# Ten slot tiles instead of twelve in a mixture-of-experts kernel: places of 96 and 64 slots, filled in the order of the token counts

## The chip, the cores and the metric

The kernel runs on one core of a Trainium2 chip. The metric is the device time of one execution in microseconds (us). Before the change three runs took 1160.12, 1155.77 and 1158.53 us, a median of 1158.53 us.

## What is computed

A two-layer transformer on 512 tokens of width 1024, float32. Each layer is attention (layer 0: block-sparse plus differential, layer 1: compressed, selected and windowed) and then a mixture of 16 experts. The change touches the mixture alone:

```python
def hier_moe(h, wg, bg, we, be, w_gate, w_up, w_down):      # t: 512 tokens x 1024
    ...
    _, gsel = lax.top_k(gl, 1)                              # one of 4 groups of 4 experts
    ...
    tv, ti = lax.top_k(el_g, MOE_TOPK)                      # 2 experts of that group
    tw = jax.nn.softmax(tv, axis=-1)
    ...
    a = jax.nn.silu(jnp.einsum('td,edf->tef', t, w_gate)) * jnp.einsum('td,edf->tef', t, w_up)
    y = jnp.einsum('tef,efd->td', a * comb[:, :, None].astype(a.dtype), w_down)
```

So 1024 (token, expert) pairs are spread over 16 experts of 256 hidden units. An expert's weights are 3 MiB: 1 MiB gate, 1 MiB up, 1 MiB down.

## The kernel before

Both layers run the same program for the mixture (`Moe.run`). Each expert has a place of `CAP` = 96 slots; the 16 x 96 = 1536 slots are cut into 12 slot tiles of 128 rows, that is four quarters of 32 rows each, so a tile holds rows of two experts (quarter q of tile t belongs to expert (4t + q) // 3, `groups`). For a tile t the steps are:

- `place_tile` (one-hot matrices on VectorE at L1310, small matmuls at L1317 and L1321, `indices`): which token sits in which slot. Then `gather` (L1232, GpSimd) fetches the 128 token rows from DRAM; the first tile is built by matmuls instead (`r0`, L1340).
- `normed_rows` (ScalarE, L1248) scales the rows into `xs`, `rows_T` transposes them on TensorE (L1259) into `xT`.
- `up` (L1269): 8 steps over the width and in each step four matmuls, one per quarter, each against gate and up of that quarter's expert. A whole `up`, 32 matmuls in the program, is one row of 64 in the trace. `silu` and product give `sg` (L1272, L1275).
- `down`: `sg` transposed (L1282), 16 matmuls (L1291, a row of 32 in the trace), the rows times the tokens' weights (`tile_weight`, L1404; L1294), and `scatter` (L1302, GpSimd) to the DRAM array `yD`. The last two tiles do not scatter: their rows are added by matmuls with the transposed one-hots (`combine`, L1549). `add_rows` reads `yD` back (`yr`, SP, L1534) and adds it (L1538, L1539).

TensorE runs them as: up(t+1), placing of a later tile, down(t). The order on each engine is chosen by a scheduler at build time, not written out; the program only gives the order of emission and some pins.

The weights come by DMAs that SP issues (`Experts`): per expert four half-MiB DMAs for gate and up (L1059) and one of 1 MiB for down (L1065). There are buffers for `GUB` = 5 experts of gate and up, in two halves, and for `DNB` = 4 experts of down. A buffer is free when the last matmul that reads it is done: SP then waits at that DMA, and everything behind it in SP's queue waits too.

If an expert has more than 96 tokens, the kernel runs `overflow` for it (L1416 on) inside an If (L1474) between up(2) and up(3), `IF_AT` = 2. Every engine loads the largest count, `cmaxi`, and branches. In this execution the body of that branch was not run.

Of the kernel before, what the change touches and what calls it, by code (L numbers as in the profile page):

```python
# [25 lines left out]
SLOT_TILES = NEXP * CAP // 128  # L26
# [11 lines left out]
IF_AT = 2  # L38
TAIL_AT = 8
# [35 lines left out]
def hybrid_kernel(ctx: ExitStack, tc: tile.TileContext, A: dict, out: bass.AP, dbg=None):  # L75
# [970 lines left out]
    class Experts:  # L1046


        def __init__(self, pool, l):
            self.pool, self.l, self.gu, self.dn = pool, l, {}, {}  # L1050
# [11 lines left out]
        def down(self, e):  # L1062
            if e not in self.dn and e < NEXP:
                self.dn[e] = self.pool.tile([128, 2, D], F32, name="dn", tag="dn", bufs=DNB)
                nc.sync.dma_start(self.dn[e], A["moe_w_down"][self.l, e].rearrange("(p j) c -> p j c", j=2))  # L1065
# [106 lines left out]
    def moe(l, m, done):  # L1172
        s2, b2, nD, yD = m.s2, m.b2, m.nD, m.yD
        with mkpool(f"mx{l}") as mp, mkpool(f"moe{l}", "right") as fp:
# [9 lines left out]
            for j in range(XGB):  # L1184
# [3 lines left out]
            PIECES = {0: ((0, 0, 0, 96), (1, 0, 96, 32)), 1: ((1, 32, 0, 64), (2, 0, 64, 64)),  # L1188
                      2: ((2, 64, 0, 32), (3, 0, 32, 96))}
            SPAN = {0: (0, 2), 1: (1, 3), 2: (2, 4)}  # L1190
# [5 lines left out]
            for h in range(2):  # L1196
# [7 lines left out]
                for i in range(2 * h, 2 * h + 2):  # L1204
                    for e, s0, o, n in PIECES[0]:
# [12 lines left out]
            for q in (1, 2):  # L1218
                nc.gpsimd.tensor_tensor(rsr, rs[:, :NT] if q == 1 else rsr, rsp[:, :, q - 1], op=ALU.subtract)
                nc.gpsimd.tensor_copy(rsp[:, :, q], rsr)  # L1220

# [84 lines left out]
            def place_tile(t, pinned=False):  # L1306
                b, j = t // 3, t % 3
                OH[t] = fp.tile([128, NT, 128], BF, name="oh", tag="oh", bufs=XGB + 3)
                for e, s0, o, n in PIECES[j]:
                    nc.vector.tensor_tensor(OH[t][:, :, o:o + n],  # L1310
                                            rm[:, :, 4 * b + e:4 * b + e + 1].to_broadcast([128, NT, n]),
                                            iotas[:, None, s0:s0 + n].to_broadcast([128, NT, n]), op=ALU.is_equal)
                lo, hi = SPAN[j]
                cd = cod[:, :, 4 * b + lo:4 * b + hi]
                tb = ps("P" if t in PLB else "O")
                for i in range(NT):
                    o = nc.tensor.matmul(tb[:, 0:8], OH[t][:, i, :], cd[:, i].rearrange("p e c a -> p (e c a)"),  # L1317
# [3 lines left out]
                    nc.tensor.matmul(tb[:, 8:11], OH[t][:, i, :], rsp[:, i, :], start=False, stop=(i == NT - 1),  # L1321
                                     skip_group_check=True)
                IX[t] = sm([128, 2], f"ix{t}", I32)
                indices(tb[:, 0:8].rearrange("p (e c a) -> p e c a", e=2, c=2), IX[t], segm[:, j, lo:hi])
                RSL[t] = sm([128, 1], f"rsl{t}")
                nc.vector.tensor_reduce(RSL[t], tb[:, 8:11], axis=AX.X, op=ALU.add)
# [49 lines left out]
            for q in range(3):  # L1376
                nc.vector.tensor_copy(wc[:, :, :, q], wv)
                if q < 2:
                    nc.vector.tensor_tensor(wv, wv, wc[:, :, :, q], op=ALU.subtract)
            cmax = sm([128, 1], "cmax")  # L1380
# [305 lines left out]
```

## Time and profile before

| | |
|---|---|
| median of 3 runs | 1158.53 us |
| the profiled execution | 1158.82 us |
| its span, first to last instruction | 1157.1 us |
| mean granted TensorE clock | 0.963 |
| TensorE busy | 1056.2 us, 91% |
| mixture of layer 0, first `up` to the last `down` | 369.05 to 528.96 us |
| mixture of layer 1, first `up` to the last `down` | 976 to 1139.3 us |

The profiled execution was 1158.82 us, of which 1.72 us lie outside the span. Times in the trace count from the span's start. A row of a timeline gives start, duration, engine, line, operation, out<-in, count, and in brackets the idle time before it with what ended it. Busy TensorE is measured in matmuls whose ends are modelled, so the starts are what is read here. An engine name with a q behind it is that engine's own instruction queue.

### The profile page before, as it was taken

The page shows a single profiled execution, that of the slowest core. Times are in us where ns is not written, and L with a number is a line of the kernel's source. Part 1 is how long each engine was busy: PE and PEld are TensorE (multiplying, and loading weights), DVE is VectorE, ACT ScalarE, POOL GpSimd, SP SyncE. Part 2 cuts the span into 40 slices and gives each one's busy share as a digit, 9 for nine tenths or more (in the row PEclk, how much of TensorE's full clock was granted, in tenths as well). Part 3 has the DMA queues.
Part 4 walks back from the last instruction along what each step waited for, and adds up shares of the span by engine and source line. Part 5 has one row for each costly group of instructions (what it writes and reads, how often), then busy time and mean ns, then how long its engine had stood idle before and what let it go on. Part 6 is the DMA issues. An engine that isn't in the chain of part 4 may idle for free. (4 is left out here: it accounts for less than half of the span.)

```text
span 1157.1 us, 21456 instructions
## 1 busy us (share of the span) xinstructions
PE 1056.2 (91%) x8123; PEld 729.7 (63%) x8124; DVE 598.9 (52%) x1651; ACT 512.5 (44%) x1277; POOL 275.9 (24%) x355
## 2 busy tenths in 40 slices
PE   5899899989998999996999997995999998999994
PEld 3798889978773433334999976763678673433332
DVE  2575869775325332338327587547564225332337
ACT  3235565765442222224334674674755542313222
POOL 2110011332222211212101242233324323211214
PEclk9989999999998999998999998998999998999997
DMA  8864647541196889855376265005012094989853
GB/s 272 293 191 147 200 147 225 196 147 56 55 382 212 310 328 412 329 190 166 76 192 227 79 202 173 15 16 139 27 37 74 12 396 183 309 336 416 319 202 125
DMA packets 114212, 225.98 MB, mean 195 GB/s; under 512 B 31694, under 2 KB 75662, under 8 KB 108976
## 3 DMA queue, kind: packets, MB, share of 16 engines
q1 hardware_dynamic: 104832, 203.85, 51.4%
q0 software_dynamic: 7776, 20.07, 4.6%
q8 instruction: 68, 1.11, 0.4%
q10 hardware_dynamic: 1488, 0.55, 0.2%
q14 instruction: 48, 0.39, 0.1%
HBM read 212.73 MB, written 18.93 MB: 200 GB/s over the span
## 5 line engine op out<-in xcount | busy, mean ns | idle before, releaser
L343 PE MATMUL psP<-wh,hTh 128*128 128x256 f32 (+1 forms) x656 | 190.1, 295 | 12.1 <-ACT raw L456 6.3
L343 PE MATMUL psP<-wl,hTh 128*128 128x256 f32 (+1 forms) x656 | 184.8, 292 | 6.5 <-DVE wl L312 6.4
L343 PE MATMUL psP<-wh,hTl 128*128 128x256 f32 (+1 forms) x656 | 187.9, 290 | 0.1
L1269 PE MATMUL psS<-gu,xT 128*32 128x512 f32 x1536 | 175.9, 603 | 0.3
L343 PEld LDWEIGHTS psP<-wh,hTh 128*128 128x128 f32 x656 | 128.3, 197 | 15.1 <-ACT raw L456 7.1
L343 PEld LDWEIGHTS psP<-wl,hTh 128*128 128x128 f32 x656 | 125.5, 195 | 9.8 <-DVE wl L312 8.9
L509 DVE CUSTOM_DVE_ANT_0 P<-psS,cmask 128x128 f32<-128x128 f32 x192 | 87.3, 487 | 85.7 <-PE psS L505 51.8
L518 POOL TENSOR_SCALAR P<-P,sm 128x128 f32<-128x128 f32 (+3 forms) x160 | 94.3, 609 | 150.2 <-DVE sm L957 72.2
L343 PEld LDWEIGHTS psP<-wh,hTl 128*128 128x128 f32 x656 | 127.7, 195 | 3.4 <-issue 2.5
L310 ACT CAST wh<-w 128x512 fp32r<-128x512 f32 (+1 forms) x124 | 75.2, 608 | 116.7 <-PE psP L343 74.7
L510 ACT ACTIVATE P<-P,nm 128x128 f32<-128x128 f32 x192 | 107.4, 561 | 37.6 <-DVE nm L509 37.1
L312 POOL TENSOR_TENSOR wl<-w,wh 128x512 fp32r<-128x512 f32 (+1 forms) x38 | 52.5, 1383 | 283.2 <-ACT wh L310 236.2
L1269 PEld LDWEIGHTS psS<-gu,xT 128*32 128x32 f32 x1536 | 55.3, 111 | 99.7 <-issue 90.9
L234 DVE SCALAR_TENSOR_TENSOR g<-w,cs,g 128x512 f32<-128x512 f32 x140 | 111.0, 818 | 11.0 <-DMA w<-in_ada_w_dram 11.0
L505 PE MATMUL psS<-kT,qT 128*128 128x256 f32 (+3 forms) x384 | 95.7, 345 | 3.1 <-DVE nm L509 2.7
L343 PE MATMUL psP<-wh,o 128*128 128x256 f32 x480 | 94.1, 289 | 2.1 <-ACT o L310 1.4
L312 DVE TENSOR_TENSOR wl<-w,wh 128x512 fp32r<-128x512 f32 (+1 forms) x86 | 59.6, 693 | 67.9 <-ACT wh L310 67.1
L1291 PE MATMUL psP<-dn,sT 128*32 128x512 f32 x768 | 89.1, 603 | 1.0 <-ACT sT L1284 0.8
L173 ACT COPY PT<-psT 128x512 f32<-128x512 f32 x132 | 66.1, 511 | 46.7 <-PE psT L531 46.0
L343 PEld LDWEIGHTS psP<-wh,o 128*128 128x128 f32 x480 | 75.1, 190 | 13.3 <-issue 8.2
L531 PE MATMUL psT<-identr,P 128*128 128x128 f32 x440 | 72.5, 284 | 5.0 <-ACT PT L173 4.8
L1240 ACT ACTIVATE xT<-psT,bm,sm 128x128 f32<-128x128 f32 x96 | 36.1, 457 | 88.8 <-PE psT L1259 88.8
(338 smaller groups left out, 1729.0 us busy)
## 6 DMA issues: line engine op xcount, KB each, us to landing
w<-in_ada_w_dram SPq DMA_DIRECT2D x96, 512.0 KB
gu<-in_moe_w_gate_dram SPq DMA_DIRECT2D x64, 512.0 KB
gu<-in_moe_w_up_dram SPq DMA_DIRECT2D x64, 512.0 KB
dn<-in_moe_w_down_dram SPq DMA_DIRECT2D x32, 1024.0 KB
w<-in_ev_w_in_dram SPq DMA_DIRECT2D x20, 512.0 KB
w<-in_od_w_in_dram SPq DMA_DIRECT2D x18, 512.0 KB
yr<-yD SPq DMA_DIRECT2D x8, 1024.0 KB
w<-in_ev_w_out_dram SPq DMA_DIRECT2D x8, 512.0 KB
```

The source lines that it names most:

```text
L173: nc.scalar.copy(o, i)
L234: nc.vector.scalar_tensor_tensor(g1[:, h], t[:, h], cs[:, k:k + 1], g1[:, h], op0=ALU.mult, op1=ALU.add)
L310: nc.scalar.copy(hi, src)
L312: o = e.tensor_tensor(lo, src, hi.bitcast(F32), op=ALU.subtract)
L343: nc.tensor.matmul(dst, xx[:, k, tk], ww, start=(k == 0 and v == 0 and i % per == 0), stop=(k == 4 * len(qs) - 1 and v == 2), skip_group_c ...
L505: nc.tensor.matmul(s[:, :n], qh[:, i * 128:(i + 1) * 128], kh[:, v, :n], start=(v == 0), stop=(v == 1))
L509: nc.vector.tensor_tensor_reduce(e, s[:, :n], cmask[:, 512 - n:], -1.0, -MASKED, ALU.add, ALU.min, nm)
L510: nc.scalar.activation(e, e, AF.Exp, bias=nm, scale=-1.0, accum_out=sm[:, i:i + 1])
L518: nc.gpsimd.tensor_scalar(P[i], P[i], sm[:, i:i + 1], 1.0, op0=ALU.mult, op1=ALU.mult)
L531: nc.tensor.transpose(t[:, o:o + 128], P[i][:, j * 128:(j + 1) * 128], ident)
L1269: nc.tensor.matmul(hp[c], xT[:, k, c], gu(k), start=(k == 0), stop=(k == KC - 1), tile_position=(0, 32 * q))
L1291: nc.tensor.matmul(yp[g], sT[:, f, g], dn(f, c), start=(f == 0), stop=(f == 1), tile_position=(0, 32 * q))
```

## The change

The first five experts keep a place of 96 slots (`FIXED`). The other eleven are sorted by token count on VectorE at run time and put into eleven places whose sizes are fixed: ranks 1 to 3 get 96 slots, ranks 4 to 11 get 64, in the order of `RANKS`. 8 x 96 + 8 x 64 = 1280 slots are 10 tiles. Since the expert of a place past the fifth is only known at run time, SP loads its number (`values_load`) and the weight DMAs take their address from that register. One-hots, codes and weights of the tokens are put into the new order by products with the permutation (`reorder`). The If asks whether any place overflows and stands between up(7) and up(8) instead of between up(2) and up(3).

```diff
-SLOT_TILES = NEXP * CAP // 128
+FIXED = 5
+RANKS = (4, 5, 1, 6, 7, 2, 8, 3, 9, 10, 11)
+NSORT = NEXP - FIXED
+CAPS = (96,) * FIXED + tuple(96 if r <= 3 else 64 for r in RANKS)
+GROUPS = [(p, s) for p, n in enumerate(CAPS) for s in range(0, n, 32)]
+SLOT_TILES = len(GROUPS) // 4
+LATER = 100
...
-IF_AT = 2
-TAIL_AT = 8
+IF_AT = 7
+TAIL_AT = 6
...
+        def src(self, n, e):
+            if e < FIXED:
+                return A[n][self.l, e]
+            if e not in self.at:
+                self.at[e] = nc.values_load(self.ids[0:1, e:e + 1], engines=[mybir.EngineType.SP], min_val=FIXED,
...
+            return A[n][self.l, bass.ds(self.at[e], 1)].rearrange("o a b -> (o a) b")
...
-                        v = A[n][self.l, e].rearrange("(p k) f -> p k f", k=KC)
+                        v = self.src(n, e).rearrange("(p k) f -> p k f", k=KC)
...
+            def reorder(out, v):
+                n = v.shape[1]
+                t = row_tile()[:, 0:n * NSORT * NSORT].rearrange("p (i r e) -> p i r e", r=NSORT, e=NSORT)
+                nc.vector.tensor_tensor(t, ordr[:, None, :, :].to_broadcast([128, n, NSORT, NSORT]),
+                                        v[:, :, None, :].to_broadcast([128, n, NSORT, NSORT]), op=ALU.mult)
+                nc.vector.tensor_reduce(out, t, axis=AX.X, op=ALU.add)
+
+            def order():
+                nc.vector.tensor_copy(cnt, rk[:, 64:80])
+                nc.vector.scalar_tensor_tensor(key, cnt[:, FIXED:], float(NEXP), num, op0=ALU.mult, op1=ALU.subtract)
...
+            def reordered():
+                nc.gpsimd.tensor_copy(rmP[:, :, 0:FIXED], rm[:, :, 0:FIXED])
+                reorder(rmP[:, :, FIXED:], rm[:, :, FIXED:])
...
             def place_tile(t, pinned=False):
-                b, j = t // 3, t % 3
+                lo, hi, pieces, seg = place_of(t)
+                r, cods = (rm, cod) if hi <= FIXED else (rmP, codP)
...
             def groups(t):
-                return [weights((4 * t + q) // 3) for q in range(4)]
+                return [weights(expert_of(t, q)) for q in range(4)]
...
-                with tc.If(rv > CAP):
+                with tc.If(rv > 0):
...
             sg = up(xT0, groups(0), pinned=True)
+            with ahead(-LATER):
+                order()
+                reordered()
+                reorder_weights()
+                beyond()
...
                 if t == IF_AT:
-                    for e in range(GUB):
-                        weights.gate_up(4 * (t + 1) // 3 + e)
-                    for e in range(DNB):
-                        weights.down(4 * t // 3 + e)
+                    for e in range(done_by(t) + GUB):
+                        weights.gate_up(e)
+                    for e in range(done_by(t - 1) + DNB):
+                        weights.down(e)
```

The places of the ten tiles, quarter by quarter, are 0 0 0 1, 1 1 2 2, 2 3 3 3, 4 4 4 5, 5 6 6 7, 7 7 8 8, 9 9 10 10, 10 11 11 12, 12 12 13 13 and 14 14 15 15, counting tiles from 0. The first four tiles use 1.33 experts each; from tile 4 on it is about 1.8. The number of DMAs and of bytes of weights is unchanged.

What moves on the engines is shown at three places. First SP's queue at the start of the mixture of layer 0. The name `gu` is a half of gate and up (two halves to an expert, each with a gate and an up DMA), `dn` a down matrix. Before, with the fifth expert's `gu_4846` first and `dn_4870`, `dn_4872` those of experts 4 and 5:

```order
L1473 TENSOR_LOAD cmaxi_4464
L1059 DMA gu_4846<-in_moe_w_gate_dram 128x1024
...
L1059 DMA gu_4852<-in_moe_w_gate_dram 128x1024
...
L1065 DMA dn_4870<-in_moe_w_down_dram 128x2048
L1059 DMA gu_4858<-in_moe_w_gate_dram 128x1024
...
L1059 DMA gu_4864<-in_moe_w_gate_dram 128x1024
...
L1065 DMA dn_4872<-in_moe_w_down_dram 128x2048
L1474 COMPARE_AND_BRANCH
```

And with the change, from the load of the expert numbers on (`gu_4926` is expert 5, `dn_4924` and `dn_4935` are experts 4 and 5, `gu_5056` is expert 6, `gu_5067` expert 7):

```order
L1064 TENSOR_LOAD ids_4358
L1076 ISA
L1076 DMA gu_4926<-in_moe_w_gate_dram 128x1024
...
L1570 TENSOR_LOAD cmaxi_4365
L1570 ISA x2
L1082 DMA dn_4924<-in_moe_w_down_dram 128x2048
...
L1082 DMA dn_4935<-in_moe_w_down_dram 128x2048
...
L1076 DMA gu_5056<-in_moe_w_gate_dram 128x1024
...
L1082 DMA dn_5065<-in_moe_w_down_dram 128x2048
...
L1076 DMA gu_5067<-in_moe_w_gate_dram 128x1024
```

Before, gate and up of experts 6, 7 and 8 stand ahead of the down matrix of expert 5; now expert 6 stands behind it, expert 7 behind the down matrix of expert 6, and so on, one after the other to expert 12.

Second, VectorE between the last copy of the first tile's rows and its transposed rows `xT`. Before (`ix1_4393` is the index of tile 1, which its gather waits for):

```order
L1340 COPY w_4330<-psS_4329 128x256
...
L1228 TENSOR_REDUCE t2_4396<-t4_4394 128x2
L1229 TENSOR_SCALAR ix0_4373<-t2_4376 128x2
...
L1229 TENSOR_SCALAR ix1_4393<-t2_4396 128x2
...
L1243 TENSOR_SCALAR xT_4327<-psT_4343,sm0_3296,bm0_3302 128x128 x4
```

With the change (`ix1_4432` is that of tile 1):

```order
L1438 COPY w_4369<-psS_4368 128x256
L1294 TENSOR_TENSOR ordr_4359<-rank_4357,want_4295 128x121
...
L1283 TENSOR_TENSOR w_4562<-ordr_4359,rm_4316 128x484
...
L1283 TENSOR_TENSOR w_4567<-ordr_4359,eb_4343 128x484
...
L1283 TENSOR_TENSOR w_4571<-ordr_4359,wv_4476 128x484
L1285 TENSOR_REDUCE key_4356<-w_4557 128x11
L1342 TENSOR_SCALAR xT_4366<-psT_4382,sm0_3296,bm0_3302 128x128 x4
...
L1285 TENSOR_REDUCE rmP_4361<-w_4562 128x4x11
...
L1285 TENSOR_REDUCE ebP_4566<-w_4567 128x44
L1328 TENSOR_SCALAR ix1_4432<-t2_4435 128x2
```

The index of tile 1 stood ahead of `xT` and now stands behind it and behind three of the reductions; three products of 484 elements and the sort stand ahead of `xT`.

Third, TensorE around up(4) with the change, where the scheduler has cut it (L1368 is `up`, L1381 and L1390 are the transposes and matmuls of `down`):

```order
L1358 MATMUL psT<-identr,xs 128x128 x4
L1368 MATMUL psS<-gu,xT 32x512 x3
...
L1381 MATMUL psT<-identr,sg 128x128 x2
...
L1390 MATMUL psP<-dn,sT 32x512 x16
...
L1368 MATMUL psS<-gu,xT 32x512 x18
...
L1368 MATMUL psS<-gu,xT 32x512 x13
```

Before, every `up` ran through; now three matmuls (those of experts 5, 6 and 6) come ahead of down(3), and the fourth, of expert 7, comes behind it. The same cut stands ahead of experts 8, 10 and 12.

## Rows read from the trace of the kernel before

**Rows 1.** The page, busy time, share of the span and instructions of each engine.

```profile
PE 1056.2 (91%) x8123; PEld 729.7 (63%) x8124; DVE 598.9 (52%) x1651; ACT 512.5 (44%) x1277; POOL 275.9 (24%) x355
```

**Rows 2.** TensorE's timeline, layer 0: `up`, `down` and the weights' matmuls.

```profile
369.05 7.14 PE L1269 MATMUL psS<-gu,xT 128*32 128x512 f32 x64
...
377.44 7.17 PE L1269 MATMUL psS<-gu,xT 128*32 128x512 f32 x64
...
390.10 7.07 PE L1269 MATMUL psS<-gu,xT 128*32 128x512 f32 x64
406.39 0.24 PE L1404 MATMUL psO<-wc,oh 128*128 128x6 bf16 x4 [3.76 <-PEq L1474]
406.65 8.78 PE L1269 MATMUL psS<-gu,xT 128*32 128x512 f32 x64
...
420.73 7.07 PE L1269 MATMUL psS<-gu,xT 128*32 128x512 f32 x64
...
433.11 7.07 PE L1269 MATMUL psS<-gu,xT 128*32 128x512 f32 x64
...
499.94 3.62 PE L1269 MATMUL psS<-gu,xT 128*32 128x512 f32 x26
```

**Rows 3.** Busy time by stretch: PE, PEld, DVE, ACT, POOL, granted clock, DMA share, GB/s.

```profile
402.00:414.00 12.00, 8.22 (x64) 3.56 (x68) 1.65 (x5) 2.65 (x5) 1.01 (x1) 0.86 0.95 376
414.00:420.00 6.00, 6.00 (x66) 2.33 (x58) 3.60 (x14) 0.76 (x2) 1.02 (x1) 1.00 0.41 113
420.00:474.00 54.00, 54.00 (x516) 19.96 (x516) 16.69 (x55) 15.75 (x33) 11.01 (x11) 1.00 1.02 407
```

**Rows 4.** SP's timeline, layer 0, the issues of weights.

```profile
381.11 0.33 SPq L1059 DMA_DIRECT2D gu<-in_moe_w_gate_dram  x1
...
402.02 0.33 SPq L1065 DMA_DIRECT2D dn<-in_moe_w_down_dram  x1
...
420.17 0.90 SPq L1065 DMA_DIRECT2D dn<-in_moe_w_down_dram  x2
...
481.89 0.33 SPq L1065 DMA_DIRECT2D dn<-in_moe_w_down_dram  x1
```

**Rows 5.** VectorE's timeline, layer 0, routing and the first tile.

```profile
354.08 0.57 DVE L1164 TENSOR_TENSOR c<-c,c_k_tri 128x320 f32<-128x320 f32 x1
354.69 0.48 DVE L1165 TENSOR_REDUCE place<-c 128x80 f32<-128x320 f32 x1
...
368.12 0.16 DVE L1229 TENSOR_SCALAR ix<-t 128x2 int32<-128x2 f32 x1
...
368.58 1.37 DVE L1243 TENSOR_SCALAR xT<-psT,sm,bm 128x128 f32<-128x128 f32 x4 [0.17 <-PE psT L1259]
...
376.64 0.42 DVE L1275 TENSOR_TENSOR sg<-sg,psS 128x256 f32<-128x256 f32 x1 [6.62 <-ACT sg L1272]
```

**Rows 6.** The timelines of POOL and ACT: the gather of tile 1.

```profile
368.58 1.16 POOL L1232 DMA_INDIRECT xg<-nD,ix  x1 [12.74 <-DVE t L1228]
...
373.46 1.15 ACT L1248 ACTIVATE xs<-xg,rsl 128x1024 f32<-128x1024 f32 x1 [2.88 <-DMA xg<-nD,ix]
```

**Rows 7.** The end of the mixture of layer 0, all engines' timeline.

```profile
509.20 0.97 POOL L1302 DMA_INDIRECT yD<-w,ix  x1 [12.81 <-DVE w L1294]
...
512.42 1.97 SPq L1534 DMA_DIRECT2D yr<-yD  x4
513.29 7.05 PE L1269 MATMUL psS<-gu,xT 128*32 128x512 f32 x64
...
525.32 3.64 PE L1291 MATMUL psP<-dn,sT 128*32 128x512 f32 x32
...
528.26 1.28 DVE L1539 TENSOR_TENSOR X<-X,yr 128x512 f32<-128x512 f32 x2
...
532.37 0.69 DVE L1553 TENSOR_TENSOR X<-psS,X 128x512 f32<-128x512 f32 x1
```

**Rows 8.** TensorE's timeline, layer 1, at the If.

```profile
1014.44 8.69 PE L1269 MATMUL psS<-gu,xT 128*32 128x512 f32 x64
```

More of the change, by code (lines that the diff above doesn't have):

```diff
@@ L1187, in moe, with place_of, expert_of, done_by @@
             OH, IX, RSL = {}, {}, {}
-            PIECES = {0: ((0, 0, 0, 96), (1, 0, 96, 32)), 1: ((1, 32, 0, 64), (2, 0, 64, 64)),
-                      2: ((2, 64, 0, 32), (3, 0, 32, 96))}
-            SPAN = {0: (0, 2), 1: (1, 3), 2: (2, 4)}
+            PIECES = ((0, 0, 0, 96), (1, 0, 96, 32))
+            seg4 = sm([128, 3], "seg4")
+            nc.gpsimd.memset(seg4, 0.0)
+            for q, e in enumerate((0, 1, 1, 2)):
+                nc.gpsimd.memset(seg4[32 * q:32 * q + 32, e:e + 1], 1.0)
+            caps, want = sm([128, NEXP], "caps"), sm([128, NSORT], "want")
+            nc.gpsimd.memset(caps, float(min(CAPS)))
+            for p in range(NEXP):
+                if CAPS[p] == CAP:
+                    nc.gpsimd.memset(caps[:, p:p + 1], float(CAP))
+            for j, r in enumerate(RANKS):
+                nc.gpsimd.tensor_copy(want[:, j:j + 1], iotas[:, r - 1:r])
+            def place_of(t):
+                g = GROUPS[4 * t:4 * t + 4]
+                lo, hi = g[0][0], g[3][0] + 1
+                pieces = []
+                for p in range(lo, hi):
+                    q = [j for j in range(4) if g[j][0] == p]
+                    pieces.append((p, g[q[0]][1], 32 * q[0], 32 * len(q)))
+                form = tuple(p - lo for p, _ in g)
+                if form == (0, 1, 1, 2):
+                    return lo, hi, pieces, seg4
+                j = {1: 0, 2: 1, 3: 2}[sum(form)]
+                return lo, hi, pieces, segm[:, j, j:j + 2]
+            def expert_of(t, q):
+                return GROUPS[4 * t + q][0]
+            def done_by(t):
+                return expert_of(t + 1, 0) if t + 1 < SLOT_TILES else NEXP
             rm = sm([128, NT, NEXP], "rm")
@@ L1320, in place_tile @@
                         pin(o)
-                    nc.tensor.matmul(tb[:, 8:11], OH[t][:, i, :], rsp[:, i, :], start=False, stop=(i == NT - 1),
+                    nc.tensor.matmul(tb[:, w:w + 3], OH[t][:, i, :], rsp[:, i, :], start=False, stop=(i == NT - 1),
                                      skip_group_check=True)
                 IX[t] = sm([128, 2], f"ix{t}", I32)
-                indices(tb[:, 0:8].rearrange("p (e c a) -> p e c a", e=2, c=2), IX[t], segm[:, j, lo:hi])
+                indices(tb[:, 0:w].rearrange("p (e c a) -> p e c a", c=2, a=2), IX[t], seg)
                 RSL[t] = sm([128, 1], f"rsl{t}")
-                nc.vector.tensor_reduce(RSL[t], tb[:, 8:11], axis=AX.X, op=ALU.add)
+                nc.vector.tensor_reduce(RSL[t], tb[:, w:w + 3], axis=AX.X, op=ALU.add)
                 if t > 0:
@@ L1375, in moe, with reorder_weights @@
             wc = sm([128, NT, NEXP, 3], "wc", BF)
[L1376 to L1380, printed above, removed]
-            nc.vector.tensor_reduce(cmax, rk[:, 64:80], axis=AX.X, op=ALU.max)
-            cmaxi = sm([128, 1], "cmaxi", I32)
-            nc.vector.tensor_copy(cmaxi, cmax)
-            cnti = sm([128, NEXP], "cnti", I32)
-            nc.vector.tensor_copy(cnti, rk[:, 64:80])
+            def reorder_weights():
+                reorder(wt[:, :, FIXED:], wv[:, :, FIXED:])
+                nc.vector.tensor_copy(wv[:, :, FIXED:], wt[:, :, FIXED:])
+                for q in range(3):
+                    nc.vector.tensor_copy(wc[:, :, :, q], wv)
+                    if q < 2:
+                        nc.vector.tensor_tensor(wv, wv, wc[:, :, :, q], op=ALU.subtract)
             g2 = g1
```

67 lines of the change are left out of this document (49 added, 18 removed).

## The prediction, made before the changed kernel was run

> **What bounds the kernel now.** I read the totals first, then TensorE's timeline through the mixture, then the stretches, then SP's queue. TensorE is busy 91% of the span [rows 1]. In the mixture the starts of `up` lie 12.38 us apart (420.73, 433.11) and nothing stands between them but work [rows 2]: a tile costs its matmuls, 7.07 us for `up`, 3.64 for `down` [rows 7], the rest transposes and placing. The one hole is the If: 3.76 us of idle, and behind it an `up` of 8.78 instead of 7.07 [rows 2], because the granted clock was 0.86 in that stretch, so part of it ran at 1.2 instead of 2.4 GHz [rows 3]. So a stop of TensorE of that length costs 1.71 us on top; layer 1 shows the same (8.69) [rows 8].
>
> The second thing to see is that the transfers are full as well. From 420 to 474 us their share is 1.02 at 407 GB/s while TensorE is busy 54.00 of 54 us [rows 3]. Twelve tiles with 1.33 experts each just match the two. Nobody waits, so a change that makes one of them faster makes the other the bound.
>
> **Two tiles less.** A tile has the same matmuls whichever places are mixed in it. Two tiles of 12.38 us are 24.76 us of TensorE per layer, 49.5 in all. That is the whole gain; everything else is cost.
>
> **The start.** Three products of 484 elements and the sort stand ahead of `xT`. A product of 320 took 0.57 us [rows 5], so 0.86 each or 2.6 us; the products and reductions of 121 elements I put at 0.2 each, 0.6 together; about 1.0 us of small work moves behind. So up(0) starts 2.2 us later. The index of tile 1 is done at 368.28 and its gather issued at 368.58 now [rows 5, 6]. It comes to stand behind `xT` (1.37), and behind two reductions of 484 (a reduction of 320 took 0.48, so 0.73 each) and smaller work of about 0.7: 368.58 + 2.2 + 1.37 + 1.46 + 0.7 = 374.3, or 5.7 us later. The rows reach ScalarE 4.88 us after the issue (373.46) [rows 6], and from there to up(1) it was 3.98 us (377.44) [rows 2]; TensorE was busy all that time. With the change up(1) can start at 374.3 + 4.88 + 3.98 = 383.2, or some earlier, since the transfers are emptier then. I take 5.0 us later, 382.5; its ends are 2.2 (only up(0) late) and 5.8. TensorE then stands still for some 3 us, and I add the 1.71 for the clock. The other small work (POOL's constants, the branch's counts) costs nothing: VectorE has 6.62 us of idle there [rows 5]; were that cover gone, `sg` of tile 0 would be late by the 2 or 3 us it is over.
>
> **SP's queue.** Before, SP issues gate and up of expert 6 at 381.11, as soon as up(1) frees the buffer, and the down matrix of expert 5 at 402.02, when down(1) ends [rows 4]. With the change expert 6 stands behind that down matrix, so nothing is issued between; the engines run empty for some 20 us, as they did at 414 to 420, where SP stood at the If, at 113 GB/s [rows 3]. No one misses expert 6 before up(4). But that lead is what the later tiles lived on: from tile 4 on a tile takes 1.8 experts of 3.15 MB and one gather and one scatter of 0.52 MB, 6.7 MB in 12.38 us. That is 540 GB/s, against the 407 of [rows 3].
>
> Now by time, layer 0. up(3) follows up(1) by 25.45 us, without the If (406.65 - 3.76 - 377.44) [rows 2], plus 1.71: 409.7. up(4) follows by 12.38 at 422.0 and down(2) ends 0.7 before, at 421.3. There the down matrix of expert 6 is issued, and from there the queue hardly runs dry. Until up(7) can run its fourth matmul (expert 12; the scheduler cut it off there) it must bring six down matrices (6 to 11, 6.3 MB), gate and up of 7 to 11 (10.5 MB), the first half of 12 (1.05 MB) and seven gathers and scatters (3.7 MB): 21.5 MB, at 407 GB/s 52.8 us, so 474.1 and with a landing of about 1 us 475. TensorE without a stall would be there at 422.0 + 3 x 12.38 + about 5 for down(6), which is put ahead: 464. So about 11 us are stalls at experts 7, 10 and 12, in up(4), up(6) and up(7).
>
> From 475: the rest of up(7) is 6.4 us and 1.71 for the clock, 483.1. The If costs its 3.76 as before and 0.3 for the weights: 487.2; POOL stands there too, but all gathers are issued ahead of it and one scatter, that of tile 7, behind it. up(8) at the low clock is 8.78: 496.0. From there to the end of the last down it is as before from the end of up(10), 503.56, to 528.96 [rows 2, 7], 25.4 us: 521.4. So **TensorE ends 7.5 us earlier** of the 24.76.
>
> **The tail.** The scatter of the third tile from the end went out at 509.20 and its result is read back from 512.42 [rows 7]. With the change that tile's down(7) stands just behind the If, and the rows cannot be used before SP has passed it, which it does when all it issued has landed: 10.5 MB behind the first half of expert 12, 25.8 us, at 501. down(7) ends at about 501 too, its scatter goes out at about 504, 5 earlier, and has the last two down matrices (2.1 MB, 5.2 us) beside it; half of that is 2.6. The adds ended 2.83 us before the combine began (529.54, 532.37) [rows 7], so up to that delay is hidden: a gain of 5.0 to 5.3 by this chain and 7.5 by TensorE's. I take 6 for the start of the next layer. Two layers are 12 us: 1158.82 - 12 = 1146.8 for the profiled execution, which is 0.29 above the median; **1146.5 us** against 1158.53.
>
> The Trainium skill (DMA: Bandwidth & Descriptors, Specifications) gives a limit of about 358 GB/s of HBM per core and a fabric ceiling of 435. Row [rows 3] shows 407 over 54 us, so the first does not hold here. By the second, the 540 GB/s that the late tiles would need could not be had either.
>
> **The rivals.**
>
> *TensorE stays the bound.* The start costs 6.7 and nothing stalls: 24.76 - 6.7 = 18 per layer, 1158.8 - 36 = 1122.8. For it: no wait of TensorE on weights in the mixture of before, and buffers for five experts. Against it: the transfers are full already [rows 3]. Chance 0.15.
>
> *The queue runs dry (slower).* My sum has the engines busy from 421 on. But SP stands at every down matrix until the `down` of TensorE four experts earlier ends, and TensorE now waits for SP's transfers: each may wait for the other in turn. If the engines stand empty for 12 us in these 52, as they did for much of 414 to 420 [rows 3], expert 12 lands at 487, two of the three stops cost their 1.71 as well, and the sum is 7.5 - 12 - 3.4 = 8 us lost per layer: 1174. The point is 7.5 us empty per layer. Against it: what SP can issue by 430 (down of 6 to 8, gate and up of 7 to 9, 9.4 MB) lasts the engines 23 us, to 444, and the down(4) that frees the next down matrix ends about 442. Chance 0.14.
>
> *The stream is slower with addresses from registers.* No row shows such a transfer. The nearest lower rate is 376 GB/s [rows 3]: 57.2 instead of 52.8 us, and 6 - 4.4 = 1.6 per layer: 1155.6. By the 358 of the Trainium skill (same page, same section) it would be 60.1 us, 1.3 lost per layer and 1161.4. Chance 0.10.
>
> *The tail gives it back.* The scatter waits for both last down matrices and the adds run later than the combine: 2 to 3 us gained per layer: 1153 to 1155. Chance 0.06.
>
> *It does not do what it says: the branch runs.* Counted from the reference's own routing, the fourth in rank past the fifth has 63 tokens in layer 0, for 64 slots, so the branch should stay out by one token. If it runs, an expert is 3.15 MB (7.7 us) and a tile (12.38): at least 1167. Chance 0.05.
>
> **The numbers.** The forecast has 0.50; its own range is 1139 to 1154, from the start's ends (3.2 us better, 0.8 worse per layer) and from a landing or an idle engine of 2 to 4 us per layer. About 0.5% (5.8 us) can be told from no change. Faster by more: 0.45 of the forecast and the 0.15 of the first rival, 0.60. Within: 0.05, 0.10 and 0.06, 0.21. Slower: 0.14 and 0.05, 0.19. The range goes from 1128 (most between the first rival and the forecast) to 1167 and leaves out the lower end of the first rival, the upper part of the dry queue and some runs of the branch.
>
> **What would show it.** Starts of up(0) about 2 and of up(1) about 5 us later; the gather of tile 1 at about 374; gate and up of expert 6 issued at about 409, right behind a down matrix; a share near 0 before it and near 1 from 421 to 500; waits of `up` on the weights' DMAs, near 11 us per layer, in up(4), up(6) and up(7); the last down at about 521. No such waits mean the first rival. A share clearly below 1 from 421 to 475 means the dry queue; a share of 1 below 390 GB/s the slow stream; instructions of the branch's body the last one.

## The result, and the profile after

The change is slower: a median of 1168.02 us against 1159.61 us for the kernel before, 20 runs each, a ratio of 1.0063 with a 95% interval of [1.0047, 1.0079]. I had forecast 1146.5 us, so both the time and its direction were wrong.

TensorE did become shorter, as it had to with two tiles less. The busy time of the page, against [rows 1]:

```profile
PE 1023.7 (88%) x7651; PEld 719.6 (62%) x7652; DVE 595.7 (51%) x1641; ACT 500.0 (43%) x1249; POOL 271.8 (23%) x401
```

That is 32.5 us less busy time, where I had counted 49.5, and none of it is in the time. To see where it went I cut each profile by events that both kernels have on TensorE's timeline: the router's transposes of `lt`, the next layer's first transposes, and in the attention of layer 1 the third group of transposes of `pc`. "Mixtures" is the time from the router to the next layer's start (layer 0) plus that from the router to the end of the span (layer 1); the last two columns are the two halves of layer 1's attention, which the change does not touch. The first three rows are profiles of the unchanged kernel, the fourth holds the two of the change; the others belong to the experiments below, two values in a cell being two profiles. Each ratio is against runs of the kernel before that were measured beside it.

| kernel | mixtures, us | attention 1, first half | second half | median us, ratio to before |
|---|---|---|---|---|
| before | 385.6 | 268.3 | 151.8 | 1159.61 |
| before_again | 388.6 | 269.0 | 151.4 | 1164.34, one run |
| before_third | 387.8 | 269.3 | 151.4 | 1163.58, one run |
| after, after_again | 385.8, 387.1 | 269.4, 267.1 | 157.9, 157.6 | 1168.02, 1.0063 [1.0047, 1.0079] |
| start, start_again | 387.7, 387.9 | 272.0, 269.9 | 151.6, 152.4 | 1160.12, 1.0003 [0.9986, 1.0021] |
| prefetch, prefetch_again | 356.9, 361.0 | 269.3, 269.3 | 157.4, 157.7 | 1139.86, 0.9831 [0.9795, 0.9866] |
| no_last_down | 379.4 | 268.9 | 152.8 | 1150.17, 0.9904 [0.9882, 0.9927] |
| if6 | 393.5 | 270.9 | 152.5 | 1167.13, 1.0050 [1.0015, 1.0086] |
| if2 | 400.1 | 270.5 | 152.5 | 1173.01, 1.0114 [1.0069, 1.0159] |
| prefetch_start_if4 | 363.8 | 269.8 | 152.0 | 1141.76, 0.9854 [0.9817, 0.9891] |
| prefetch_start_ranks | 354.2 | 268.2 | 151.7 | 1128.28, 0.9737 [0.9688, 0.9787] |
| tail_order | 382.6 | 273.2 | 152.6 | 1157.72, 0.9977 [0.9952, 1.0001] |
| all_four | 355.2 | 269.8 | 152.5 | 1128.65, 0.9721 [0.9686, 0.9755] |

Two things stand in the first four rows. The mixtures come out even: 387.3 us as a mean of three profiles before, 386.5 as a mean of two after. And the second half of layer 1's attention takes 6 us longer.

**The mixture.** TensorE's timeline in layer 0, the rows that answer to [rows 2] and [rows 7] (columns as there; L1368 is now `up`, L1390 `down`, L1571 the If):

```profile
372.40 7.14 PE L1368 MATMUL psS<-gu,xT 128*32 128x512 f32 x64 [1.34 <-DVE xT L1342]
...
383.85 7.17 PE L1368 MATMUL psS<-gu,xT 128*32 128x512 f32 x64 [1.23 <-DVE xT L1342]
...
421.43 1.06 PE L1368 MATMUL psS<-gu,xT 128*32 128x512 f32 x6
...
433.18 5.86 PE L1368 MATMUL psS<-gu,xT 128*32 128x512 f32 x36 [3.77 <-DMA gu<-in_moe_w_up_dram]
...
471.04 1.05 PE L1368 MATMUL psS<-gu,xT 128*32 128x512 f32 x4 [1.26 <-DMA gu<-in_moe_w_up_dram]
...
489.10 0.24 PE L1500 MATMUL psO<-wc,oh 128*128 128x9 bf16 x4 [3.52 <-PEq L1571]
489.27 8.77 PE L1368 MATMUL psS<-gu,xT 128*32 128x512 f32 x64
...
517.62 3.64 PE L1390 MATMUL psP<-dn,sT 128*32 128x512 f32 x32
```

Three stops of `up` on weights, in up(4), up(6) and up(7) (the third, 1.28 us, stands at 478.55). The last `down` ends at 521.26. In this profile the router stands 2.2 us later than in that of before (353.68 against 351.44), so times of the two are compared from there. From the router the last `down` ends at 167.6 us, and at 170.9 in the second profile; before it was 177.5. TensorE's part of layer 0's mixture is thus 7 to 10 us shorter.

The stretches, for [rows 3] (the columns are the same):

```profile
384.00:408.00 24.00, 24.00 (x244) 10.31 (x240) 9.72 (x41) 5.61 (x12) 4.80 (x5) 1.00 0.40 124
408.00:420.00 12.00, 12.00 (x122) 4.73 (x122) 4.69 (x17) 3.29 (x7) 2.24 (x3) 1.00 0.91 319
432.00:474.00 42.00, 37.74 (x310) 13.05 (x314) 9.83 (x25) 7.34 (x16) 4.89 (x5) 0.96 1.01 402
...
516.00:528.00 12.00, 5.87 (x42) 2.24 (x40) 9.51 (x11) 0.37 (x1) 5.60 (x4) 0.86 1.03 398
528.00:540.00 12.00, 7.02 (x20) 5.30 (x20) 8.58 (x14) 5.92 (x17) 0.38 (x2) 0.71 0.38 95
```

Read the share of the DMA engines' time that was busy, in the second column from the right: 0.40 while TensorE has its weights, 1.01 while it waits for them. The reason is in SP's timeline, for [rows 4]; the first row is the two down matrices at which SP stands, the next two gate and up of expert 6 behind them:

```profile
395.89 12.87 SPq L1082 DMA_DIRECT2D dn<-in_moe_w_down_dram  x2
409.29 0.33 SPq L1076 DMA_DIRECT2D gu<-in_moe_w_gate_dram  x1
409.81 1.01 SPq L1076 DMA_DIRECT2D gu<-in_moe_w_up_dram  x1
```

Now the end of the layer, for [rows 7], on all engines:

```profile
504.06 0.97 POOL L1401 DMA_INDIRECT yD<-w,ix  x1 [25.36 <-DVE w L1393]
511.98 2.28 SPq L1636 DMA_DIRECT2D yr<-yD  x4
...
527.71 1.28 DVE L1641 TENSOR_TENSOR X<-X,yr 128x512 f32<-128x512 f32 x2
528.91 0.74 DVE L1393 SCALAR_TENSOR_TENSOR w<-psP,sw,g 128x512 f32<-128x512 f32 x1
530.35 1.65 PE L1651 MATMUL psS<-xg,oT 128*128 128x512 f32 x3 [8.43 <-ACT xg L1628]
...
541.81 0.69 PE L330 MATMUL psT<-identr,nrm 128*128 128x128 f32 x2 [4.44 <-DVE nrm L314]
```

The scatter goes out at 504.06 instead of 509.20, but its rows are read back at 511.98 instead of 512.42, and the adds end at 528.99 instead of 529.54. Counted from the router the scatter is 7.4 us earlier, the read 2.7 and the end of the adds 2.8 (5.4, 1.2 and 0.7 in the second profile of the change). The row behind them is the one to look at. It weights the rows of the last `down`, whose matmuls were done at 521.26, and it stands behind the adds in VectorE's queue. So it starts at 528.91, and the combine, which needs these rows, waits 8.43 us. In the kernel before this row was as late; there `down` itself had only just ended (528.96). Its row, the start of the combine and the stretch from 528 to 540 us in the kernel before:

```profile
529.46 0.74 DVE L1294 SCALAR_TENSOR_TENSOR w<-psP,sw,g 128x512 f32<-128x512 f32 x1
530.90 0.97 PE L1549 MATMUL psS<-xg,oT 128*128 128x512 f32 x3 [1.28 <-ACT xg L1526]
528.00:540.00 12.00, 6.73 (x34) 3.94 (x26) 9.48 (x16) 7.29 (x20) 1.59 (x5) 0.99 0.41 109
```

From the end of the last `down` to the next layer it was 11.5 us and is 20.5: most of what TensorE gained it stands idle. The work behind the wait is dearer as well: the granted clock, the third column from the right, was 0.71 from 528 to 540 us and 0.99 before, and from the first matmuls behind the wait to the next layer it takes 11.5 us (11.1 in the second profile) instead of 9.55. In layer 1 it is much the same: the last `down` ends 168.6 and 169.1 us from the router, where it was 178.8 to 181.7, the combine waits 8.8 and 8.7 us, and the end comes at 197.7 and 197.3 us, where it was 196.6 to 199.5.

**The attention.** The second half of layer 1's attention in the kernel after (the whole of it, and 20 us of it; columns as in [rows 3]),

```profile
811.19:969.13 157.94, 149.81 (x955) 106.49 (x955) 65.58 (x204) 88.88 (x242) 51.34 (x76) 0.97 0.31 114
831.00:851.00 20.00, 15.01 (x93) 11.36 (x93) 13.42 (x28) 9.40 (x24) 3.91 (x6) 0.83 0.16 54
```

and in the kernel before:

```profile
808.74:960.49 151.75, 147.12 (x956) 105.68 (x956) 66.07 (x204) 87.98 (x242) 51.60 (x76) 0.99 0.33 122
828.00:848.00 20.00, 18.48 (x122) 12.10 (x122) 13.26 (x32) 13.36 (x34) 4.64 (x7) 1.00 0.18 55
```

It is the same work. After has 3.5 us more idle time on TensorE (157.94 - 149.81 against 151.75 - 147.12) and 2.7 us more busy time at a lower clock. The place, on VectorE and TensorE, after:

```profile
832.58 0.81 DVE L320 TENSOR_TENSOR qst<-raw,qst 128x256 fp32r<-128x256 f32 x1 [1.04 <-ACT qst L318]
834.34 5.37 DVE L370 TENSOR_TENSOR w<-w,g 128x512 f32<-128x512 f32 x7 [0.95 <-DMA g<-modg]
839.63 0.41 DVE L320 TENSOR_TENSOR qst<-raw,qst 128x256 fp32r<-128x256 f32 x1
...
840.10 0.75 PE L472 MATMUL psT<-identr,qst 128*128 128x128 f32 x4 [3.62 <-DVE qst L320]
```

and before, where L312 is the same line:

```profile
831.58 0.43 DVE L312 TENSOR_TENSOR qst<-raw,qst 128x256 fp32r<-128x256 f32 x1 [1.88 <-ACT qst L310]
832.06 0.53 PE L464 MATMUL psT<-identr,qst 128*128 128x128 f32 x4 [0.61 <-DVE qst L312]
832.71 7.18 DVE L362 TENSOR_TENSOR w<-w,g 128x512 f32<-128x512 f32 x10 [0.70 <-DMA g<-modg]
```

Before, VectorE did the second `qst` ahead of ten products for the next weights, so TensorE waited 0.61 us for it. After, seven of these products stand ahead of it, and TensorE waits 3.62 us. No line of the diff is in this code. What is left is the build-time scheduler, which arranged it anew when the program ahead of it had changed.

### The profile page after: what moved, and what is told of

The parts are those of the page before. It is cut to its first block, busy times and chain, and to the rows that moved or that the text cites. A ratio compares the mean times of both kernels' runs of the same rounds, so it can differ in the third digit from the quotient of the medians.

```text
span 1166.8 us, 20700 instructions
## 1 busy us (share of the span) xinstructions
PE 1023.7 (88%) x7651; PEld 719.6 (62%) x7652; DVE 595.7 (51%) x1641; ACT 500.0 (43%) x1249; POOL 271.8 (23%) x401
## 5 line engine op out<-in xcount | busy, mean ns | idle before, releaser
L1368 PE MATMUL psS<-gu,xT 128*32 128x512 f32 x1280 | 155.8, 620 | 16.8 <-DMA gu<-in_moe_w_up_dram 11.7
L1368 PEld LDWEIGHTS psS<-gu,xT 128*32 128x32 f32 x1280 | 48.1, 114 | 105.9 <-issue 95.0
L351 PEld LDWEIGHTS psP<-wh,o 128*128 128x128 f32 x480 | 75.6, 192 | 11.7 <-issue 5.7
L1390 PE MATMUL psP<-dn,sT 128*32 128x512 f32 x640 | 73.2, 596 | 2.8 <-DVE w L1393 1.7
L513 PEld LDWEIGHTS psS<-kT,qT 128*128 128x128 f32 x384 | 60.6, 192 | 22.2 <-DVE nm L517 9.4
## 6 DMA issues: line engine op xcount, KB each, us to landing
dn<-in_moe_w_down_dram SPq DMA_DIRECT2D x32, 1024.0 KB, 13.3
```

The lines of the kernel that those rows point to most:

```text
L351: nc.tensor.matmul(dst, xx[:, k, tk], ww, start=(k == 0 and v == 0 and i % per == 0), stop=(k == 4 * len(qs) - 1 and v == 2), skip_group_c ...
L513: nc.tensor.matmul(s[:, :n], qh[:, i * 128:(i + 1) * 128], kh[:, v, :n], start=(v == 0), stop=(v == 1))
L1368: nc.tensor.matmul(hp[c], xT[:, k, c], gu(k), start=(k == 0), stop=(k == KC - 1), tile_position=(0, 32 * q))
L1390: nc.tensor.matmul(yp[g], sT[:, f, g], dn(f, c), start=(f == 0), stop=(f == 1), tile_position=(0, 32 * q))
```

## The experiments

Two questions: what costs the 8.4 us, and what eats the two tiles. For the first my theory was the order of the attention, with noise between runs as its rival. For the second it was SP's queue (a down matrix ahead of each next expert), with the tail and the start as rivals.

**start: the start undone.** The sort's late part is held back until the index of tile 2 is written, so the index of tile 1 stands ahead of it again:

```diff
...
-            with ahead(-LATER):
+            with ahead(-LATER), tc.issue_after(IXO[2].ins):
```

> The change, but the sort and all that follows from it stand behind the index of tile 2 on VectorE, so the gather of tile 1 goes out as early as before. By building it this way the scheduler also gives the attention of both layers exactly the order of the kernel before. Three theories of the 9.7 us that the profile of the change lost. (1) Attention: 7.3 us of it are lost in layer 1's attention (first transposes to router: 420.0 before, 427.3 with the change) because the scheduler ordered it otherwise; then this kernel takes 420 there. (2) It is scatter between runs; then 424 to 430 or anything else. (3) Tail: in the mixture TensorE's last down is 7.7 us earlier, but the adds of the rows read back end no earlier. Then the start (router to up(1) 26.0 before, 30.2 with the change) should come back to 26 to 27 here and still give the mixture at most 1 or 2 us per layer. Total by (1) and (3): 1158 to 1161. By (1) and a mixture that follows TensorE: 1150 to 1154.

Measured: a ratio of 1.0003 [0.9986, 1.0021], some 7 us less than the change. But the mixtures of its two profiles, 387.7 and 387.9 us, are no shorter than the 385.8 and 387.1 of after. What went away is the second half of the attention:

```profile
814.94:966.59 151.65, 147.19 (x955) 105.68 (x956) 66.11 (x204) 87.96 (x242) 51.63 (x76) 0.99 0.32 118
```

By the lists of the engines' orders this stretch is in `start` instruction for instruction that of the kernel before. So the start as such costs nothing at the mixture's end, and the gain is the order of a stretch that neither edit touches. No run changes that order alone; the repeats below ask whether the tie holds.

**prefetch: the weights asked for ahead.** The two loops that ask for the weights of the next experts stood under `if t == IF_AT`, so they ran for one tile. Here they run for every tile, which puts gate and up ahead of the down matrices in SP's queue again:

```diff
+                for e in range(done_by(t) + GUB):
+                    weights.gate_up(e)
+                for e in range(done_by(t - 1) + DNB):
+                    weights.down(e)
                 if t == IF_AT:
-                    for e in range(done_by(t) + GUB):
-                        weights.gate_up(e)
-                    for e in range(done_by(t - 1) + DNB):
-                        weights.down(e)
```

> The change, but the lines that ask for gate, up and down weights ahead of time are run at every tile and not only at the If, so gate and up of experts 6, 7 and 8 stand ahead of the down matrix of expert 5 again in SP's queue. Attention is ordered as with the change. Queue theory (the forecast's): TensorE's waits on gate and up in the mixtures, 11.7 us in all, fall below 3, and the last down comes 4 to 7 us earlier in each layer. Tail theory: the end of the mixture moves by the scatter of tile 7 and the reads behind it, and since the stream of weights also ends earlier this moves 3 to 6 us per layer; total 1156 to 1162. If the transfers as such are the bound (all bytes at 407 GB/s) the last down moves less than 2 us and the total stays at 1166 to 1168. Attention of layer 1 should take 427 again by theory (1) of the run with the start undone.

Measured: 0.9831 [0.9795, 0.9866]. The stretches of its layer 0:

```profile
384.00:408.00 24.00, 24.00 (x248) 10.07 (x244) 9.66 (x38) 6.06 (x14) 6.03 (x6) 1.00 0.92 322
...
432.00:474.00 42.00, 38.57 (x350) 14.06 (x346) 12.69 (x36) 10.87 (x24) 7.30 (x8) 1.00 1.02 420
```

The share from 384 to 408 us goes from 0.40 to 0.92, no wait of `up` on weights is left, and the two mixtures are 28 us shorter (359.0 as a mean, 387.3 before). So SP's queue did hold back most of what two tiles less can give. But it is not what made the change slower than before, since even with it the mixtures were as long as before. The wait at the combine is untouched (waited for, us in total, times, longest):

```profile
PE psS L1651 <- ACT xg L1628: 16.7, 2, 8.7
```

**no_last_down: the tail without transfers beside the scatter.** Experts 14 and 15 use the down matrices of 12 and 13, so the kernel leaves out the last two loads and computes something else:

```diff
+            if e in (14, 15):
+                self.dn[e] = self.dn[e - 2]
```

> The change, but the down matrices of experts 14 and 15 are not loaded (those of 12 and 13 are used for them). Tail theory: with the change the scatter of tile 7 took 7.9 us from its issue to the read (504.06 to 511.98), where before it was 3.2, because these two matrices, 2.1 MB, stand beside it; without them it lands in 3 to 5 us, the reads go out at 507 to 509, the adds end 3 to 4 us earlier and the next layer starts 3 to 4 earlier. Rival: the adds themselves (VectorE and GpSimd) or the reads are the slow part; then the end of the mixture moves less than 1 us. The attention of layer 1 has a third order here, its time is not forecast.

Measured: 0.9904 [0.9882, 0.9927]; the mixtures are 7 us shorter than after. POOL's scatter, SP's read of its rows and the combine behind them:

```profile
508.37 0.97 POOL L1403 DMA_INDIRECT yD<-w,ix  x1 [25.82 <-DVE w L1395]
511.72 1.94 SPq L1638 DMA_DIRECT2D yr<-yD  x4
...
530.43 0.96 PE L1653 MATMUL psS<-xg,oT 128*128 128x512 f32 x3 [1.62 <-ACT xg L1630]
```

It goes out 4.3 us later than after and is read 0.3 us earlier: 3.35 us from issue to read instead of 7.92, as in the kernel before (3.22). The combine's wait of 8.43 us falls to 1.62. TensorE's last `down` ends 173.1 us from the router here, later than after's 167.6 and 170.9, and layer 0's mixture is still 3 to 5 us shorter: the tail sets its end, not TensorE. How much of the 7 us is the landing, and how much simply 2 MiB less to load, is not separated by this run.

**if6: the branch one tile earlier.** `IF_AT = 6` instead of 7.

> The change with the If between up(6) and up(7) instead of up(7) and up(8). The attention is ordered as before but for four places in TensorE's queue. Theory (1): attention of layer 1 takes 420 to 421; if the 7.3 us were scatter, any value from 420 to 428. In the mixture SP now passes the If ahead of the last gate and up (expert 15), which then has less lead: TensorE waits 2 to 6 us at the last tile, and the mixture is 1 to 4 us longer per layer than with the change. Total 1162 to 1168.

Measured: mixtures 2.5 (layer 0) and 4.5 us (layer 1) longer than the means of after, with a wait of 2.14 us on weights in the last `up` of layer 0; 1.0050 [1.0015, 1.0086]. The attention is in the order of before (152.5), so the total stays close to after's. The place at the seventh tile is no loss; it is the better of the two.

**if2: the branch where it was.** `IF_AT = 2`, so only the place of the If is undone.

> The change with the If where it was before, between up(2) and up(3); nothing else. SP's queue is then gate and up 5, 6, down 4, gate and up 7, 8, down 5, the If, and after it down and gate and up in turn. If it was the move of the If that took the lead of the weights away, TensorE's waits on gate and up (11.7 us in all with the change) fall to 5 or less, the last down is 170 or so from the router less 3 to 6, and the total is 1155 to 1163. If pairs of down and gate and up as such are the cause, wherever the If stands, the waits stay at 8 to 14 us.

Measured: 1.0114 [1.0069, 1.0159], the slowest of all. TensorE's waits in the mixture of `if2`,

```profile
PE psS L1368 <- DMA gu<-in_moe_w_up_dram: 13.5, 7, 4.6
```

and of the kernel after (waited for, us in total, times, longest):

```profile
PE psS L1651 <- ACT xg L1628: 17.2, 2, 8.8
PE psS L1368 <- DMA gu<-in_moe_w_up_dram: 11.7, 5, 3.8
```

One theory falls here: that the If, being late, took away the moment at which SP asked for many weights at once. With the If at its old place the waits are 13.5 us, against 11.7 and 13.3 in the two profiles of after. The loss of lead lies in the order of SP's queue behind the If: gate and up, then down, expert by expert. By the source I read it so: loads whose address is in a register stay in the order of the program, while those of the kernel before, with fixed addresses, could be moved ahead by the scheduler. That is argued from the lists of orders; no run separates it.

**prefetch_start_if4 and prefetch_start_ranks: what a better version needs.** Both have the edits of `prefetch` and `start`. The first also has `IF_AT = 4`; the second puts the two late places of 96 slots last:

```diff
-RANKS = (4, 5, 1, 6, 7, 2, 8, 3, 9, 10, 11)
+RANKS = (4, 5, 1, 6, 7, 8, 9, 10, 11, 2, 3)
```

> As prefetch, with the sort behind the indices, and the If between up(4) and up(5). Attention exactly in the order of before: 420 to 424 us by the attention theory, 427 if the order does not matter. In the mixture SP waits at the If for all it has issued, in the middle of the stream, which leaves the transfer engines without work for 2 to 4 us; TensorE has a lead of two to three experts there, so by the queue theory this costs nothing or up to 2 us per layer against prefetch, and the start gives 2 to 4 back. Scatter of tile 7 still beside 2 MiB: about 8 us. Total 1128 to 1137.

> Weights asked for ahead at every tile (as in the run prefetch, 1139.9), the sort behind the indices (as in the run start), and the places of the second and third in rank moved to the end of the list, so that the last tile holds two experts of which only one has its down matrix loaded at the end: 1 MiB beside the scatter of tile 7 instead of 2. Attention nearly in the order of before. Tail theory: the scatter of tile 7 takes 5 to 6 us to the reads instead of 8.0; the mixture is 2 to 3 us per layer shorter than in prefetch (174.9 and 182.0) from this, and 2 to 4 more from the start, now that neither the queue nor the stream of weights hides it. Attention theory: 420 to 424 instead of 426.8. Total 1122 to 1132. If the start is hidden behind the transfers as in the run start: 1130 to 1136.

Measured: 0.9854 [0.9817, 0.9891] and 0.9737 [0.9688, 0.9787]. With the earlier If the mixtures are 3 to 7 us longer (363.8 against 356.9 and 361.0 of `prefetch`), about what the attention's order gives back; the two profiles of `prefetch` lie 4 us apart, so this is likely and not shown. With the other ranks it is the best version, 1128.28 us, faster than both kernels. Against `prefetch` that is 11.6 us: 5.9 in the attention's second half and 4.8 in the mixtures. No run has `prefetch` and `start` alone, so the ranks and the start are not separated in the 4.8. With these ranks the last tile brings in one expert instead of two, and one down matrix instead of two stands beside the last scatter. That scatter in `prefetch_start_ranks`,

```profile
486.29 0.98 POOL L1401 DMA_INDIRECT yD<-w,ix  x1 [17.02 <-DVE w L1393]
...
492.26 1.99 SPq L1636 DMA_DIRECT2D yr<-yD  x4
```

and in `prefetch`, where two stand beside it:

```profile
488.20 0.98 POOL L1401 DMA_INDIRECT yD<-w,ix  x1 [15.76 <-DVE w L1393]
...
496.23 2.27 SPq L1636 DMA_DIRECT2D yr<-yD  x4
```

From issue to read, in layer 0, it is 3.35 us with nothing beside it (`no_last_down`), 5.97 with 1 MiB and 8.03 with 2 MiB.

**tail_order: the last `down` ahead of half the adds.** Two of the four row groups are added before the last `down`, two behind it, so the weighting of its rows can come earlier on VectorE:

```diff
-            for i in ROWS:
+            for i in ROWS[:2]:
                 add_rows(i)
...
+            for i in ROWS[2:]:
+                add_rows(i)
```

> The change, but the last two of the four reads of scattered rows are asked for and added behind the last down in the program, so that on VectorE the weighting of the last down's rows stands between the adds and no longer behind all of them; the attention comes out nearly in the order of before. Theory: with the change the weighting ran at 528.91, 7.7 us after the last down had ended at 521.26, only because it stood behind the adds. Here it should start at 524 to 526, TensorE's wait of 8.8 us at the combine fall to 3 to 6, and the mixture be 1 to 3 us shorter per layer (188.1 and 197.7 with the change), since VectorE has the same work to do in the end. If the mixture stays as long, the late reads alone set its end. Attention of layer 1 420 to 424. Total 1155 to 1161.

Measured: 0.9977 [0.9952, 1.0001], mixtures 3.8 us shorter than after (382.6). The wait of the combine in the kernel `tail_order`:

```profile
PE psS L1651 <- ACT xg L1628: 7.7, 2, 5.3
```

So 9.5 of 17.2 us of waiting go away and 3.8 arrive at the end, all of it in layer 1 (192.9 us instead of 197.7 and 197.3); layer 0 has 189.7, as after (188.1 and 189.8). The rest is taken up, at least in part: the other adds now stand between the combine's rows on VectorE, and the combine waits for other rows 3.3 us more (0.85 of them at 537.26). That the weighting stood behind the adds was a cost of the change, but a re-ordering alone does not bring the tail's loss back.

**all_four: `prefetch_start_ranks` with `tail_order`.**

> The kernel of the run prefetch_start_ranks (1128.3) with the same exchange on VectorE. There the waits at the combine were 2.8 us and at the product of the last tile 4.2. If VectorE's total work sets the end, nothing changes: 1126 to 1130. If the place of the weighting counts: 1 to 2 us per layer, 1124 to 1127.

Measured: 0.9721 [0.9686, 0.9755] against 0.9737 [0.9688, 0.9787], no difference that can be told. With one down matrix beside the scatter the tail has too little left to win.

**The repeats.** The kernel before twice more, and after, `prefetch` and `start` once more, for the attention's second half.

> The kernel before once more, for the scatter of its stretches between executions: router of layer 0 at 351.4, mixture 189.0, attention of layer 1 420.0, second mixture to the end 196.6. Attention theory: 419 to 422 again. If it comes out at 424 or more, the 7.3 us of the change are half scatter.

> The change once more. If the order of layer 1's attention costs time: 425 us or more there. If it is scatter: any value from 420 to 426.

> The run prefetch once more, with the same order of attention as the change. By order: 425 us or more in layer 1's attention. By scatter: any value from 420 to 426.

> The run start once more, whose attention has exactly the order of before. By order: 420 to 424 us in layer 1's attention. By scatter: as likely above 425 as below.

> The kernel before a third time. By order: 420 to 424 us in layer 1's attention. By scatter: as likely above 425 as below.

Measured: the four profiles with the change's order in this stretch (after and `prefetch`, twice each) have 157.4 to 157.9 us, the twelve others 151.4 to 152.8. The wait for the second `qst` is 3.5 or 3.6 us in those four and 0.6 in eleven of the others (2.0 in two pieces in `start_again`). The first half goes from 267.1 to 273.2 us without any tie to the order. So the 6 us go with the order in every profile, and the first half is noise.

## Why the prediction was wrong

By steps, against the forecast's own numbers, counted from the router where the two kernels are compared.

- **Two tiles less.** Right in kind: 49.5 us were counted; TensorE's busy time is 32.5 us less in the change and 44.1 in the first profile of `prefetch`, where the weights are on time and the two mixtures lose 28 us. The granted clock (0.946 and 0.957, before 0.963) is likely part of the difference; it is not taken apart.
- **The start.** The mechanism was right and it does not reach the end. The products of 484 elements took 0.66 us each (0.86 forecast). Forecast were 2.2 us for up(0) and 5.0 for up(1); up(0) is 1.1 us later in one profile and not later in the other, up(1) 4.2 and 3.1. The clock's 1.71 came in one of the two: up(1) took 7.17 us in the first and 8.69 in the second, behind a stop of the same length. Undoing the start gave the mixture nothing: it is hidden behind the transfers and the tail.
- **SP's queue.** Right in its places. Expert 6 was issued at 409.29, right behind a down matrix (the share ahead of it was 0.40, where I had said near 0), and the stops were in up(4), up(6) and up(7). The stops were 6.3 us in layer 0 and 11.7 in both (13.3 in the second profile), where I forecast 11 a layer. up(4) began at 421.43; from the router that is 2.8 us earlier than the 422.0 of the forecast. The way between the stops was longer: from 421.43 to 478.55 without its stops 50.8 us, where I counted 42. Of this the clock of 0.96 is some 1.7 us over 42 and two waits for VectorE 1.7; the rest I have not taken apart. The "landing of about 1 us" in this sum has no row of its own. These errors nearly cancel, which is luck: the last `down` ends 167.6 and 170.9 us from the router, and the forecast of 521.4 is 170.0.
- **The slow stream, the dry queue, the branch.** Not what happened. Register-addressed loads ran at 402 GB/s at a share of 1.01, and no row of the branch's body is in the trace. By the Trainium skill (DMA: Bandwidth & Descriptors, Specifications) about 358 GB/s is the limit of HBM per core; the trace does not agree, here as little as before.
- **The tail: the step that failed.** "The adds ended 2.83 us before the combine began (529.54, 532.37) [rows 7], so up to that delay is hidden". There was no such slack in layer 0. Between the adds and the combine stands VectorE's weighting of the last `down` (529.46), in the same queue behind the adds; TensorE's combine began at 530.90, and 532.37 is VectorE's add of its first result. I read a gap between two ends as slack without asking what the engine did in it, and I read it in layer 0 alone. The second error is in the same step: of the two down matrices beside the scatter I counted half, 2.6 us more. The landing went from 3.2 to 7.9 us (7.5 in the second profile), 4.3 to 4.7 more, nearly the whole time of the 2 MiB (5.2 us at 407 GB/s). The third is a term at nothing: TensorE's stop at the combine got no cost of the clock, though I had charged 1.71 us for a stop at the If; behind it the way to the next layer took 1.5 to 1.9 us more. So of a scatter 7.4 us earlier from the router 2.8 remain at the end of the adds and 0.9 at the next layer (second profile: 5.4, 0.7 and 0.8 lost), where I took 6. The mixtures gain 0.8 us together where I took 12. The rival that names this mechanism, "The tail gives it back", had 0.06, and even it left 2 to 3 us a layer.
- **What was in no step.** The order of the attention's second half: 6.0 us. It alone turns "no change" into "slower", which the kernel `start` shows, with mixtures as long as the change's and a ratio of 1.0003. I compared the orders only at the places that the change touches.

Together: 12 us were forecast as gain and 8.4 lost, 20.4 between them. 11.2 are the mixtures (12 - 0.8) and 6.0 the attention. The 3.2 left over are not located; the other stretches vary by more than that from profile to profile. The same sum fits the other kernels within about 3 us, but for `prefetch_start_if4` (1136.1 against 1141.76): for `if2`, 1159.6 + (400.1 - 387.3) = 1172.4 against 1173.01 measured, for `prefetch`, 1159.6 + (359.0 - 387.3) + 6.0 = 1137.3 against 1139.86.

## What to carry to other kernels

Before a gap between two ends is counted as slack, read what stands in that gap in each engine's queue: an instruction whose input comes early still runs at its place in the queue. Where a scheduler chooses the orders at build time, compare the order of the stretches that the diff leaves alone too, since one such stretch here was worth as much as the whole verdict. And loads whose buffers become free at different times should not alternate in one in-order queue: asking for the next experts' gate and up ahead of the down matrices was worth 28 us.

## What the runs showed of the hardware

A scatter to DRAM that is issued right behind weight loads did not share the bandwidth evenly with them here; it landed nearly behind them. In both layers of the profiles its rows could be read 3.2 to 3.4 us after the issue with no load beside it (4.55 in one case of eight), 6.0 to 6.8 with 1 MiB, and 7.5 to 8.2 with 2 MiB (9.4 and 9.6 in layer 1 of `start_again` and `start`). That is 2.1 to 3.5 us for each MiB, around the 2.58 us that a MiB takes at 407 GB/s. I had expected half of it. In `if6` and `if2` 4 MiB stand around the scatter of layer 0; 1.5 and 2.5 of them were issued ahead of it, and it took 7.6 and 8.8 us. So it is the loads ahead of it that seem to count; that is read from two runs made for another question.

The granted clock fell again behind an idle stretch of TensorE: 8.43 us of waiting at the end of layer 0's mixture, and 0.71 in the 12 us from 528, where TensorE was busy 7.02 us. In the attention it was 5 us of two waits, and 0.83 over the 20 us around them. A stop of the same length does not always bring it: ahead of up(1) the waits were 1.83 and 1.23 us in one profile of the change and 1.85 and 1.23 in the other, and up(1) ran at a granted clock of 1.00 in the first and of 0.82 in the second, where its row is

```profile
379.05 8.69 PE L1368 MATMUL psS<-gu,xT 128*32 128x512 f32 x64 [1.23 <-DVE xT L1342]
```
